# Wider value products, one GLU block moved, and a token-major end in a two-layer hybrid encoder

## The chip, the cores and the metric

The kernel runs on one core of a Trainium2 chip. The metric is the device time of one execution in microseconds (us). The engines are named as the profile names them: PE is TensorE's matrix products (PEld its weight loads), DVE is VectorE, ACT is ScalarE, POOL is GpSimd, SP is SyncE, whose queue issues most DMA transfers.

## The reference, cut to what matters

All is float32, with 512 tokens, width 1024 and two layers. The heads of the neighbourhood attention and the two halves of the GLU are columns of one projection.

```python
h = rmsnorm(x, norm_mix[i])
proj = h @ w_in[i]
qa, ka, va, glu_in, qc, kc, vc, gates = jnp.split(proj, SPLITS, axis=-1)
ya = diff_attention(qa, ka, va, ...)              # 4 heads of 2 x 64, values of 128
yb = conformer_conv(glu_in, ...)                  # a * sigmoid(g), 31 taps per channel, layernorm, silu
yc = neighbourhood_attention(qc, kc, vc, rpb)     # 8 heads of 64, window 8 x 16 on an 8 x 64 grid
merged = ga * (ya @ w_br_a) + gb * (yb @ w_br_b) + gc * (yc @ w_br_c)
x = x + merged @ w_o[i]
x = x + (silu(h @ w_ffn_gate[i]) * (h @ w_ffn_up[i])) @ w_ffn_down[i]     # h: normed x
x = x + sigmoid(h @ w_ple_gate[i]) * (p[i] @ w_ple_in[i])                 # h: normed x
# after both layers: rmsnorm(x, norm_final)
```

## The kernel before

Activations lie channel-major: a tile has 128 channels on the partitions and 512 tokens along them, and the width of 1024 is eight such chunks. Every product is made of three: both operands are split into a rounded high part and the rest (`split`: ACT writes `hi`, DVE writes `lo`), and PE adds hi·hi, hi·lo and lo·hi in PSUM (`mm3`, lines 175 to 177). `weights` loads 128 x 1024 raw weights over SP's queue into a `wr` buffer (two of them), and splits them into `wh` and `wl` (three each).

PE's instructions run in the order in which the program writes them. On the other engines a scheduler orders by priority; `weights` raises its own, so that loads and splits run ahead. Each engine works its queue in order. DMA transfers use eight semaphores in turn: a transfer waits until the one eight before it has landed.

The attention work is woven into the products by hand. `chunk` counts steps of a product (three products of 512 columns each), and every fourth step is a tick, about 2.7 us of PE time. `later(gen, delay, gap)` puts a piece of work on a list that starts `delay` ticks later and at least `gap` ticks after the one before; its `yield n` continues n ticks on. A `natten_unit` makes the scores of one head and half of the queries, the softmax (DVE and ACT), two ticks later the transposes, and two ticks later the attention output. `background(after, n)` puts n of the 124 convolution taps per layer (DVE, line 158, `conv_z`) behind an instruction; the numbers stand in `BG`.

A layer begins with the GLU. In layer 0 `opening` loads x and the weights of the first four blocks in pieces, after ten warm-up products (line 321), and multiplies chunk by chunk as they land. The products are made from x before its root mean square is known; DVE multiplies by the row factor (`rb`) afterwards, and `scaled` makes normalised operands (`hs`) for all later products. `glu` makes four pairs of blocks, j = 0 to 3, each a gate and a value. Then come `natten_in(pr)` for four pairs of heads (q and k, whose halves are stacked by DMA copies, `stack`, line 617), and `natten_v(g)` for two groups of four heads: `values` (lines 571 to 575) takes 128 tokens of `hs` as the stationary operand and 256 columns of weights as the moving one.

PSUM has eight banks: `mm` three, `sc` two, `tr` two, `av` one.

At the end `ple` makes eight blocks of the embedding gate. The eighth goes through `final`, in two halves of 256 tokens: products, gate, the sum of squares by products with ones, a power on POOL, and, because the output is token-major, transposes of all eight chunks. Each 128 tokens are scaled by their factor (lines 1048 and following) and stored as one transfer of 128 x 1024.

Of the kernel before, what the change touches and what calls it, by code (L numbers as in the profile page):

```python
# [20 lines left out]
P = 128  # L21
L = 2
# [8 lines left out]
CONV_W = 31  # L31
HALO = CONV_W // 2
# [13 lines left out]
PAR_L = 8 + 8 + 8 + 1 + 4 + 4 + 4 + 4 * CONV_W  # L46
PAR = L * PAR_L + 8
WARM = 10
BG = dict(glu=2, natten=3, diff=1, gatec=2, branchc=1, gateb=5, mergea=4, mergea2=2)
# [10 lines left out]
class Net:  # L60
# [99 lines left out]
    def split(self, hi, lo, src):  # L160
        self.act(hi, src, AF.Copy)
        self.tt(lo, src, hi.bitcast(F32), ALU.subtract)

    def weights(self, ap, n):
        with self.tc.high_priority(offset=min(self.w_ahead, self.tc.cur_priority - self.p0)):
            raw = self.sb("wr", [P, 1024])
            hi = self.sb("wh", [P, 1024], F32R)
            lo = self.sb("wl", [P, 1024], F32R)
            self.nc.sync.dma_start(raw[:, :n], ap[:, :n])
            self.split(hi[:, :n], lo[:, :n], raw[:, :n])  # L170
        return hi, lo
# [135 lines left out]
    def opening(self):  # L307
# [4 lines left out]
        mix = slice(0, KD)  # L312
        nc.scalar.dma_start(self.parts[:, mix], a["par"][:, mix])
# [3 lines left out]
        nc.scalar.dma_start(xc[1], a["xT"][1])  # L317
        nc.scalar.dma_start(self.parts[:, KD:], a["par"][:, KD:])
        warm = self.ps("av")
        for _ in range(WARM):  # L320
# [4 lines left out]
        raws = {"t": [self.sb("t", [P, 256]) for _ in range(4)],  # L325
                "rp": [self.sb("rp", [P, 256]) for _ in range(4)],
# [8 lines left out]
        for k in range(KD):  # L335
            if k > 1:
                nc.sync.dma_start(xc[k], a["xT"][k])
            pieces = {0: (0, 256, "t"), 2: (256, 512, "rp"), 4: (512, 1024, "e")}
            if k == 0:
                h.append(self.operand(xc[k], self.par(0, "mix", k), FIRST[0][k]))  # L340
            if k in pieces:
                c0, c1, tag = pieces[k]
                for m, (src, wh, wl, _) in enumerate(blocks):
                    raw = raws[tag][m]
                    nc.sync.dma_start(raw, src[:, c0:c1])
                    self.split(wh[:, c0:c1], wl[:, c0:c1], raw)
            if k:
                h.append(self.operand(xc[k], self.par(0, "mix", k), FIRST[0][k]))
# [62 lines left out]
    def layer(self, i, h, xsrc, xs):  # L411
# [53 lines left out]
    def glu(self, zs):  # L465
# [5 lines left out]
        for j in range(4):  # L471
# [12 lines left out]
            def value(j=j, pa=pa, sg=sg, ta=ta, z=z):  # L484
                self.tt(ta, pa, self.rb, ALU.mult)
                mid = z[:, HALO:HALO + GW, :]
                zc = self.tt(mid.rearrange("p a b -> p (a b)"), ta, sg, ALU.mult)
                nc.vector.memset(z[:, 0:HALO, 0:1], 0.0)
                nc.vector.memset(z[:, HALO + GW:, GR - 1:GR], 0.0)
                nc.vector.tensor_copy(z[:, 0:HALO, 1:GR], z[:, GW:GW + HALO, 0:GR - 1])  # L490
                nc.vector.tensor_copy(z[:, HALO + GW:, 0:GR - 1], z[:, HALO:2 * HALO, 1:GR])
# [3 lines left out]
            self.ready(value)  # L495

    def taps(self, zs, cs):

        for j, z in enumerate(zs):
# [3 lines left out]
            for d in range(CONV_W):  # L503
                w = self.par(self.i, "cw", j * CONV_W + d)
# [83 lines left out]
    def natten_in(self, pr, st, ys):  # L588
# [19 lines left out]
        for n in range(4):  # L608
            self.later(self.natten_unit(pr, n // 2, n % 2, st4, k2, st, box, ys[pr]), 5, 1)
# [10 lines left out]
    def natten_v(self, g, st):  # L620
# [3 lines left out]

        def parts(v, a):
            v = v.rearrange("p (u a b c) -> p u a b c", u=2, b=2, c=64)
            a = a.rearrange("p (u a c) -> p u a c", u=2, c=64)
            return [(v[:, u, :, u], v[:, u, :, 1 - u], a[:, u]) for u in range(2)]

        vs = self.values(self.a["w_vc"][self.i, g], parts)  # L630


        vd = self.sb("x", [P, 2, 512], F32R)
        for n, edge in enumerate((vs[1][0:64, 0], vs[0][64:P, 1])):
            for o in range(0, P, 64):
                self.nc.sync.dma_start(vd[o:o + 64, n].bitcast(F32), edge.bitcast(F32))
        st["v", g] = vs, vd

    def natten_unit(self, pr, half, u, st4, k2, st, box, y):
# [55 lines left out]
        hc = u * 256 + (pr % 2) * P  # L695
# [253 lines left out]
    def ple(self, h, x, xs, pairs):  # L949
# [4 lines left out]
        for m in range(KD - last):  # L954
# [17 lines left out]
            self.ready(gate)  # L972
            if m >= EARLY:
# [15 lines left out]
        if last:  # L989
            return self.final(h, x[KD - 1], pairs, hn, st[0])  # L990
        self.i = i + 1
        self.main_norm(st[0], (3, 2), x=x)
        return hn

    def final(self, h, x, pairs, hn, most):
# [3 lines left out]
        nc, i, m = self.nc, self.i, KD - 1  # L999
        wg = self.weights(self.a["w_pg"][i, m], 1024)  # L1000
        wi = self.weights(self.a["w_pi"][i, m], 256)
        hn.append(self.sb("h", [P, 512]))
        g = self.sb("t", [P, 512])
        sq = self.sb("t", [P, 512])
        sums = self.ps("tr", (P, 2, 4))

        def products(out, w, acts, half, ks):
            s = slice(half * 256, half * 256 + 256)
            for k in ks:
                a = acts[k] if isinstance(acts[k], tuple) else (acts[k][:, 0, :], acts[k][:, 1, :])  # L1010
                c = slice(k * P, (k + 1) * P)
                self.mm3(out, w[0][:, c], w[1][:, c], a[0][:, s], a[1][:, s],
                         k == 0, k == len(acts) - 1)

        def total(n, src, cs):
            for c in cs:
                nc.tensor.matmul(sums[:, n, c:c + 1], src[:, c * P:(c + 1) * P],
                                 self.ones[:, 0:1], start=True, stop=True)

        def turn(tag, n, c):  # L1020
            o = self.ps(tag, (P, 4, P))
            for u in range(4):
                nc.tensor.transpose(o[:, u], hn[4 * n + u][:, c * P:(c + 1) * P], self.ident)
            return o.rearrange("p a b -> p (a b)")

        def gate(pg, half):
            s = slice(half * 256, half * 256 + 256)
            self.tt(g[:, s], pg, self.rb[:, s], ALU.mult)
            self.act(g[:, s], g[:, s], AF.Sigmoid, table="sigmoid")

        def rest(pi, half):
            s = slice(half * 256, half * 256 + 256)
            self.tt(g[:, s], g[:, s], pi, ALU.mult)
            self.tt(x[:, s], x[:, s], g[:, s], ALU.add)
            self.act(sq[:, s], x[:, s], AF.Square)
            self.act(hn[m][:, s], x[:, s], AF.Copy, scale=self.par(0, "fin", m))

        def column(half):
            cs = slice(2 * half, 2 * half + 2)
            ms = self.sb("sm", [P, 2])  # L1040
            self.stt(ms, sums[:, 1, cs], 1.0 / D, part[:, cs], ALU.mult, ALU.add)
            col = self.sb("rc", [P, 2])
            nc.gpsimd.tensor_tensor(col, ms, self.power[:, 0:2], ALU.pow)
            return col

        def store(c, col, tiles):
            r = rows[c]
            nc.vector.tensor_scalar(r[:, 0:512], tiles[0], col, None, ALU.mult)
            self.act(r[:, 512:1024], tiles[1], AF.Copy, scale=col)
            nc.sync.dma_start(self.a["out"][c * P:(c + 1) * P, :], r)  # L1050

        rows = [t for _ in range(2) for t in self.parts_of("qk", [1024], 2)]
        pg = [self.ps("mm", (P, 256)), None]
        products(pg[0], wg, h, 0, range(8))
        gate(pg[0], 0)
        pi = [self.ps("sc", (P, 256)), None]
        products(pi[0], wi, pairs, 0, range(2))
        rest(pi[0], 0)
        total(0, most, range(4))
        part = self.sb("sm", [P, 4])  # L1060
        nc.vector.tensor_scalar(part, sums[:, 0, :], 1.0 / D, EPS, ALU.mult, ALU.add)
        lows = [turn("av", 0, 0), turn("tr", 0, 1)]
        pg[1] = self.ps("mm", (P, 256))
        products(pg[1], wg, h, 1, range(6))
        total(1, sq, (0, 1))
        col = column(0)
        products(pg[1], wg, h, 1, range(6, 8))
        gate(pg[1], 1)
        pi[1] = self.ps("sc", (P, 256))
        products(pi[1], wi, pairs, 1, range(2))  # L1070
        rest(pi[1], 1)
        for c in range(2):
            store(c, col[:, c:c + 1], (lows[c], turn("mm", 1, c)))
        lows = [turn("sc", 0, 2), turn("sc", 0, 3)]
        total(1, sq, (2, 3))
        col = column(1)
        highs = [turn(t, 1, 2 + c) for c, t in enumerate(("mm", "av"))]
        for c in range(2):
            store(2 + c, col[:, c:c + 1], (lows[c], highs[c]))
# [17 lines left out]
def _heads(w):  # L1097

    w = w.reshape(L, D, 2, 2, 2, 64).transpose(0, 1, 2, 4, 3, 5)
# [89 lines left out]
```

## Time and profile before

| What | Value |
|---|---|
| median of 3 runs | 1832.29 us (1831.8 to 1832.62) |
| the profiled execution | 1832.66 us |
| its span, first to last instruction | 1830.6 us |
| mean granted TensorE clock | 0.998 |
| PE / DVE / ACT busy | 1815.6 / 1190.5 / 764.8 us |
| layer 0: values of natten, first and last product | 64.4 and 120.9 us |
| last PE work | about 1824.7 us |

A row of a busy-time window reads: the window, its length, then for each engine its busy time and the number of instructions, then the granted clock as a share of full speed, the DMA engines' share, and GB/s. A row of the waits reads: engine, tile and line, who released it, total us, times, longest. A row of the timeline reads: start, duration, engine, line, operation, output<-inputs.

### The profile page before, as it was taken

What the parts mean: (1) busy time and instruction counts of PE and PEld (TensorE: products, weight loads), DVE (VectorE), ACT (ScalarE), POOL (GpSimd) and SP (SyncE); (2) the same over time, 40 slices, a digit from 0 to 9 for tenths busy, and PEclk for the clock granted to TensorE, in tenths of its full rate; (3) what the DMA queues carried; (4) which work ended last, traced back from release to release, by engine and by line L of the source; (5) the groups of instructions that cost most, each with busy time, mean ns of one, the idle gap of its engine ahead of it and who ended that gap; (6) DMA issues with size and microseconds to landing.
All of it is one profiled execution on the core that took longest, in us unless ns stands there. A gap on an engine that the chain in (4) does not pass through costs nothing.

```text
span 1830.6 us, 23574 instructions
## 1 busy us (share of the span) xinstructions
PE 1815.6 (99%) x8796; PEld 1524.3 (83%) x8796; DVE 1190.5 (65%) x1917; ACT 764.8 (42%) x1330; POOL 23.6 (1%) x56
## 2 busy tenths in 40 slices
PE   9999999999999999999999999999999999999998
PEld 7888888888888888888888888888878888888887
DVE  6888887887644434445777878888775444344455
ACT  5476555325432222233535755552353322232344
POOL 0000000000000000000000000000000000000000
PEclk9999999999999999999999999999999999999999
DMA  5565541334422232223436655322353222322232
GB/s 176 176 191 167 144 135 41 109 101 156 146 98 99 82 102 103 99 81 113 152 121 203 183 156 145 103 75 93 107 193 104 99 97 79 117 92 99 84 107 102
DMA packets 88225, 221.13 MB, mean 121 GB/s; under 512 B 12080, under 2 KB 19376, under 8 KB 88112
## 3 DMA queue, kind: packets, MB, share of 16 engines
q1 hardware_dynamic: 87536, 218.94, 37.5%
q8 instruction: 70, 1.15, 0.2%
q10 hardware_dynamic: 576, 0.69, 0.1%
q14 instruction: 43, 0.35, 0.1%
HBM read 180.79 MB, written 7.34 MB: 103 GB/s over the span
## 4 chain that ended last, share of the span: by engine, by line
PE 93%; DVE 2%; DMA 2%; ACT 2%; issue 1%; DVEq 0%; ACTq 0%; SPq 0%; POOLq 0%; POOL 0%
PE ffn_mm L175 13%; PE ffn_mm L177 13%; PE ffn_mm L176 13%; PE mergea_mm L176 2%; PE mergea_mm L175 2%; PE mergea_mm L177 2%; PE diff_sc L757 2%; PE gatec_mm L175 2%; PE gatec_mm L176 2%; PE gatec_mm L177 2%; PE ple_mm L177 2%; PE ple_mm L175 2%; PE ple_mm L176 2%; PE wo_mm L176 2%; PE wo_mm L177 2%; PE diff_mm L175 2%
## 5 line engine op out<-in xcount | busy, mean ns | idle before, releaser
L141 ACT ACTIVATE ffn_wh<-ffn_wr 128x1024 fp32r<-128x1024 f32 (+1 forms) x152 | 144.0, 949 | 513.9 <-issue 367.8
L175 PE MATMUL ffn_mm<-wo_h,ffn_wh 128*128 128x512 f32 x704 | 274.2, 390 | 0.0
L177 PE MATMUL ffn_mm<-wo_h,ffn_wl 128*128 128x512 f32 x704 | 273.9, 389 | 0.0
L176 PE MATMUL ffn_mm<-wo_h,ffn_wh 128*128 128x512 f32 x704 | 273.9, 389 | 0.0
L155 DVE TENSOR_TENSOR ffn_wl<-ffn_wr,ffn_wh 128x1024 fp32r<-128x1024 f32 (+1 forms) x152 | 164.7, 1085 | 129.2 <-ACT ffn_wh L141 129.2
L158 DVE SCALAR_TENSOR_TENSOR conv_z<-glu_z,pre_par,conv_z 128x512 f32<-128x512 f32 x240 | 179.4, 748 | 3.0
L177 PEld LDWEIGHTS ffn_mm<-wo_h,ffn_wl 128*128 128x128 f32 x704 | 132.1, 188 | 27.5
L176 PEld LDWEIGHTS ffn_mm<-wo_h,ffn_wh 128*128 128x128 f32 x704 | 132.1, 188 | 27.4
L175 PEld LDWEIGHTS ffn_mm<-wo_h,ffn_wh 128*128 128x128 f32 x704 | 132.1, 188 | 27.3
L155 DVE TENSOR_TENSOR ffn_t<-ffn_t,ffn_mm 128x512 f32<-128x512 f32 x44 | 30.3, 688 | 114.8 <-PE ffn_mm L177 114.8
L155 DVE TENSOR_TENSOR ffn_t<-ffn_mm,wo_r 128x512 f32<-128x512 f32 x44 | 30.4, 691 | 110.3 <-PE ffn_mm L177 110.3
L141 ACT ACTIVATE mergea_wh<-mergea_wr 128x1024 fp32r<-128x1024 f32 (+1 forms) x32 | 27.1, 848 | 96.6 <-PE mergea_mm L176 70.8
L175 PE MATMUL ffn_mm<-ffn_z,ffn_wh 128*128 128x512 f32 x160 | 62.2, 389 | 0.0
L176 PE MATMUL ffn_mm<-ffn_z,ffn_wh 128*128 128x512 f32 x160 | 62.2, 389 | 0.0
L177 PE MATMUL ffn_mm<-ffn_z,ffn_wl 128*128 128x512 f32 x160 | 62.2, 389 | 0.0
L175 PE MATMUL ffn_mm<-ffn_y,ffn_wh 128*128 128x512 f32 x160 | 62.2, 389 | 0.0
L176 PE MATMUL ffn_mm<-ffn_y,ffn_wh 128*128 128x512 f32 x160 | 62.2, 389 | 0.0
L177 PE MATMUL ffn_mm<-ffn_y,ffn_wl 128*128 128x512 f32 x160 | 62.2, 389 | 0.0
L141 ACT ACTIVATE diff_a<-diff_sc,diff_s 128x512 f32<-128x512 f32 x32 | 22.0, 689 | 61.8 <-DVE diff_s L848 61.8
L848 DVE TENSOR_REDUCE diff_s<-diff_sc 128x1 f32<-128x512 f32 x64 | 41.9, 685 | 5.9 <-PE diff_sc L757 5.8
L155 DVE TENSOR_TENSOR wo_x<-wo_x,ffn_mm 128x512 f32<-128x512 f32 x32 | 22.0, 687 | 31.5 <-PE ffn_mm L177 31.5
L141 ACT ACTIVATE natten_wh<-natten_wr 128x1024 fp32r<-128x1024 f32 x24 | 25.4, 1056 | 37.4 <-issue 18.0
(583 smaller groups left out, 4628.6 us busy)
## 6 DMA issues: line engine op xcount, KB each, us to landing
ffn_wr<-w_fg SPq DMA_DIRECT2D x44, 512.0 KB, 3.2
ffn_wr<-w_fu SPq DMA_DIRECT2D x44, 512.0 KB, 3.1
ffn_wr<-w_fd SPq DMA_DIRECT2D x32, 512.0 KB, 3.4
natten_wr<-w_in SPq DMA_DIRECT2D x16, 512.0 KB, 3.7
natten_b<-bias SPq DMA_DIRECT2D x32, 256.0 KB, 3.3
diff_wr<-w_in SPq DMA_DIRECT2D x16, 512.0 KB, 3.5
gatec_wr<-w_in SPq DMA_DIRECT2D x16, 512.0 KB, 4.0
gateb_wr<-w_in SPq DMA_DIRECT2D x16, 512.0 KB, 3.3
```

The lines of the kernel that those rows point to most:

```text
L141: i = self.nc.scalar.activation(out, in_, func, **kw)
L155: return self.nc.vector.tensor_tensor(out, a, b, op)
L158: return self.nc.vector.scalar_tensor_tensor(out, a, s, b, op0, op1)
L175: mm(out, wh, ah, start=first, stop=False)
L176: mm(out, wh, al, start=False, stop=False)
L177: mm(out, wl, ah, start=False, stop=last)
L757: self.nc.tensor.matmul(out, st4[:, u, qs], st[:, ks], start=n == 0, stop=n == 1)
L848: nc.vector.tensor_reduce(out=m[:, u:u + 1], in_=sc, op=ALU.max, axis=AX.X, negate=True)
```

## The change

Values: `natten_v` makes the values of all eight heads at once. For each of the eight chunks and each 128 tokens it makes products of 512 columns into four banks (two `mm`, `av`, one `sc`). The weights are laid out wide (`_wide`), and the four banks are evicted in eight splits of 256 columns. Three taps go behind each weight split.

GLU: `glu` makes three pairs. The fourth (`glu_last`) is made from `hs`, its gate between the second and third pair of heads and its value between the third and fourth, with the sigmoid read straight from PSUM. The first pair of heads is due 10 ticks after its k instead of 5.

Opening: x's first chunk is the first transfer on SP's queue. The first weight pieces have 128 and 384 columns instead of 256 and 256; the first of them goes over ACT's queue.

End: the last two blocks are token-major. For each 128 tokens, the stationary operand is the activations and the moving one is the weights of both blocks side by side (256 columns). The sum of squares of these columns is made by DVE, the gain of the two blocks is applied as a row (`gains`), and each 128 tokens are stored by two transfers, one on ACT's queue and one on SP's.

Buffers: `wr` 3 instead of 2, `t` 7 instead of 8, `r` 3 instead of 4. A constant is renamed.

```diff
-BG = dict(glu=2, natten=3, diff=1, gatec=2, branchc=1, gateb=5, mergea=4, mergea2=2)
+BG = dict(glu=2, natten=1, values=3, diff=1, gatec=2, branchc=2, gateb=4, mergea=4, mergea2=2)
...
-        self.bufs = dict(wr=2, wh=3, wl=3, h=8, qk=2, kh=2, v=4, pt=2, y=5, z=5, x=4, t=8, rp=4,
-                         e=4, a=3, r=4, ss=1, sm=8, rc=4, b=2, s=8)
+        self.bufs = dict(wr=3, wh=3, wl=3, h=8, qk=2, kh=2, v=4, pt=2, y=5, z=5, x=4, t=7, rp=4,
+                         e=4, a=3, r=3, ss=1, sm=8, rc=4, b=2, s=8)
...
+        nc.sync.dma_start(xc[0], a["xT"][0])
         nc.scalar.dma_start(self.parts[:, mix], a["par"][:, mix])
-        xc = [t for _ in range(KD // 2) for t in self.parts_of("x", [512], 2)]
-        nc.scalar.dma_start(xc[0], a["xT"][0])
         self.consts()
...
-            pieces = {0: (0, 256, "t"), 2: (256, 512, "rp"), 4: (512, 1024, "e")}
+            pieces = {0: (0, P, "t"), 1: (P, 512, "rp"), 4: (512, 1024, "e")}
             if k == 0:
+                nc.scalar.dma_start(raws["t"][0], blocks[0][0][:, 0:P])
+                nc.scalar.dma_start(xc[1], a["xT"][1])
+                nc.scalar.dma_start(self.parts[:, KD:], a["par"][:, KD:])
...
-        self.natten_v(0, sn)
+        self.natten_v(sn)
+        last = self.glu_last(zs)
         self.natten_in(1, sn, yc)
+        next(last)
         self.natten_in(2, sn, yc)
-        self.natten_v(1, sn)
+        next(last)
         self.natten_in(3, sn, yc)
...
-        for j in range(4):
+        for j in range(3):
...
+    def glu_last(self, zs):
+        self.phase = "glu"
+        sg = self.sb("t", [P, 512])
+        z = self.sb("z", [P, GW + 2 * HALO, GR])
+        self.act(sg, self.proj(OFF_GLU + CB + 3 * P), AF.Sigmoid, table="sigmoid")
+        yield
+        self.phase = "glu"
+        self.gated(z, self.proj(OFF_GLU + 3 * P), sg)
+        zs.append(z)
+        yield
...
-            self.later(self.natten_unit(pr, n // 2, n % 2, st4, k2, st, box, ys[pr]), 5, 1)
+            self.later(self.natten_unit(pr, n // 2, n % 2, st4, k2, st, box, ys[pr]), 5 if pr else 10, 1)
...
+        accs = [self.ps(t) for t in ("mm", "mm", "av", "sc")]
+        for o in range(0, KD, 2):
+            wh, wl = self.weights(self.a["w_vc"][self.i][:, o * 512:(o + 2) * 512], 1024)
+            self.background(self.low, self.bg["values"])
+            for k in (o, o + 1):
+                s = slice((k - o) * 512, (k - o + 1) * 512)
+                for t, out in enumerate(accs):
+                    hi, lo = (a[:, t * P:(t + 1) * P] for a in self.halves(self.h[k]))
+                    mm(out, hi, wh[:, s], start=k == 0, stop=False)
+                    mm(out, hi, wl[:, s], start=False, stop=False)
+                    mm(out, lo, wh[:, s], start=False, stop=k == KD - 1)
+                    self.chunk()
...
-        for m in range(KD - last):
+        for m in range(KD - 2 * last):
...
+        for t in range(4):
+            pg = self.ps("mm", (P, 256))
+            if t == 0:
+                inputs(0)
+                inputs(1)
+            products(pg, wg, h, t, range(4))
+            if t == 1:
+                chunks(0)
+            if t in (1, 2):
+                low.append(turn(places[t - 1], hn[0:4], t - 1))
+            products(pg, wg, h, t, range(4, 6))
...
+            if t:
+                chunks(t)
+            if t > 1:
+                inputs(t)
+            products(pg, wg, h, t, range(6, 8))
+            pgs.append(pg)
+            if t == 1:
+                finish(0)
+            if t:
+                finish(t)
+            if t in (1, 2):
+                store(t - 1)
+        for t in (2, 3):
+            low.append(turn(places[t], hn[0:4], t))
+            store(t)
```

In `final`, `inputs` and `products` are the products of the embedding and of the gate for 128 tokens, `chunks` and `turn` transpose finished chunks into `tr` and other banks, `finish` is the sigmoid, the gated sum, its squares and the power, and `store` scales the rows and issues the two transfers.

More of the change, by code (lines that the diff above doesn't have):

```diff
@@ L169, in weights @@
             self.nc.sync.dma_start(raw[:, :n], ap[:, :n])
[L170 removed]
+            self.low = self.split(hi[:, :n], lo[:, :n], raw[:, :n])
         return hi, lo
@@ L972, in ple @@
             self.ready(gate)
+            if last and m == 3:
+                self.gains()
             if m >= EARLY:
@@ L993, in ple, with gains @@
         return hn
-    def final(self, h, x, pairs, hn, most):
[L999 to L1008, printed above, removed]
-            for k in ks:
[L1010 to L1020, printed above, removed]
+    def gains(self):
+        o = self.ps("tr", (P, 2, P))
+        for u in range(2):
+            g = self.par(0, "fin", KD - 2 + u)
+            self.nc.tensor.transpose(o[:, u], g.to_broadcast([P, P]), self.ident)
+        self.gain = self.sb("b", [P, 2 * P])
+        self.act(self.gain, o.rearrange("p a b -> p (a b)"), AF.Copy)
@@ L1021, in turn @@
             o = self.ps(tag, (P, 4, P))
-            for u in range(4):
-                nc.tensor.transpose(o[:, u], hn[4 * n + u][:, c * P:(c + 1) * P], self.ident)
+            for u, a in enumerate(src):
+                nc.tensor.transpose(o[:, u], a[:, t * P:(t + 1) * P], self.ident)
             return o.rearrange("p a b -> p (a b)")
[L1026 to L1079, printed above, removed]
+        def finish(t):
+            g = self.sb("t", [P, 256])
+            self.act(g, pgs[t], AF.Sigmoid, table="sigmoid", scale=rbs[:, t:t + 1])
+            self.tt(g, g, pis[t], ALU.mult)
+            v = self.sb("a", [P, 256])
+            self.tt(v, g, pair[t][:, 256:], ALU.add)
+            q = self.sb("t", [P, 256])
+            s = self.sb("s", [P, 1])
+            nc.vector.tensor_tensor_reduce(
+                out=q, in0=v, in1=v, scale=1.0, scalar=0.0, op0=ALU.mult, op1=ALU.add,
+                accum_out=s)
+            ms = self.sb("sm", [P, 1])
+            self.stt(ms, s, 1.0 / D, part[:, t:t + 1], ALU.mult, ALU.add)
+            col = self.sb("rc", [P, 1])
+            nc.gpsimd.tensor_tensor(col, ms, self.power[:, 0:1], ALU.pow)
+            vs.append(v)
+            columns.append(col)
@@ new lines, in store @@
+        def store(t):
+            col, two = columns[t], pair[t]
+            r, out = rows[t], self.a["out"][t * P:(t + 1) * P]
+            self.act(r[:, 0:512], low[t], AF.Copy, scale=col)
+            nc.scalar.dma_start(out[:, 0:512], r[:, 0:512])
+            self.stt(r[:, 768:], vs[t], col, self.gain, ALU.mult, ALU.mult)
+            nc.vector.tensor_scalar(r[:, 512:768], two[:, 0:256], col, None, ALU.mult)
+            nc.sync.dma_start(out[:, 512:], r[:, 512:])
+        pair, low, pgs, vs, columns = [], [], [], [], []
@@ new lines, in final, with inputs, chunks @@
+        places = ("av", "mm", "av", "sc")
+        def inputs(t):
+            pis.append(self.ps("sc", (P, 256)))
+            products(pis[t], wi, pairs, t, range(2))
+        def chunks(t):
+            pair.append(turn("tr", (hn[4], hn[5], x[0], x[1]), t))
+        pis = []
+        for t in range(4):
[10 more added lines that the diff above has]
+            if t == 1:
+                sums = self.ps("mm", (P, 4))
+                for c in range(4):
+                    mm(sums[:, c:c + 1], most[:, c * P:(c + 1) * P], self.ones[:, 0:1],
+                       start=True, stop=True)
+                part = self.sb("sm", [P, 4])
+                nc.vector.tensor_scalar(part, sums, 1.0 / D, EPS, ALU.mult, ALU.add)
+            if t:
[4 more added lines that the diff above has]
+            pgs.append(pg)
+            if t == 1:
+                finish(0)
[3 more added lines that the diff above has]
+                store(t - 1)
```

102 lines of the change are left out of this document (64 added, 38 removed).

## The prediction

> **What bounds the kernel now.** I read the page first, then PE's waits, then windows of busy time, then the timeline.
>
> ```profile
> span 1830.6 us, 23574 instructions
> PE 1815.6 (99%) x8796; PEld 1524.3 (83%) x8796; DVE 1190.5 (65%) x1917; ACT 764.8 (42%) x1330; POOL 23.6 (1%) x56
> PE 93%; DVE 2%; DMA 2%; ACT 2%; issue 1%; DVEq 0%; ACTq 0%; SPq 0%; POOLq 0%; POOL 0%
> ```
>
> PE (TensorE) is busy 99% and is 93% of the chain that ended last. So time can leave only where PE's own work shrinks, where PE waits, where its clock is low, and after its last product.
>
> PE's waits (us in total, times, longest):
>
> ```profile
> PE natten_sc L757 <- DMA natten_x<-natten_t: 2.0, 1, 2.0
> PE pre_mm L175 <- ACT pre_y L141: 1.4, 1, 1.4
> PE natten_tr L678 <- DVE natten_pt L155: 1.3, 2, 0.6
> PE natten_av L699 <- DVE natten_y L155: 0.7, 3, 0.3
> ```
>
> Busy time by window; the granted clock stands before the DMA share:
>
> ```profile
> 4.70:8.11 3.41, 2.00 (x8) 1.05 (x7) 1.73 (x5) 2.49 (x7) 0.00 (x0) 1.00 1.06 371
> 8.11:11.53 3.42, 3.42 (x10) 2.68 (x9) 3.42 (x11) 3.21 (x9) 0.00 (x0) 0.50 0.97 248
> 82.00:140.00 58.00, 55.52 (x351) 48.95 (x349) 46.90 (x118) 40.68 (x106) 1.51 (x10) 1.00 0.68 192
> 308.50:333.00 24.50, 24.50 (x121) 20.49 (x119) 22.03 (x34) 10.33 (x17) 1.39 (x1) 1.00 0.32 108
> ```
>
> PE worked only 2.00 of the 3.41 us before 8.11, and in the next 3.42 us it was granted half its clock. That window is a loss of 1.7 us.
>
> The pitch of the products, from the timeline (start, duration):
>
> ```profile
> 63.74 0.39 PE L175 MATMUL natten_mm<-glu_b,natten_wh 128*128 128x512 f32 x1
> 63.97 0.39 PE L176 MATMUL natten_mm<-glu_b,natten_wh 128*128 128x512 f32 x1
> ...
> 64.79 0.28 PE L571 MATMUL natten_mm<-natten_wh,glu_h 128*128 128x256 f32 x1
> 64.91 0.28 PE L573 MATMUL natten_mm<-natten_wl,glu_h 128*128 128x256 f32 x1
> 65.03 0.28 PE L575 MATMUL natten_mm<-natten_wh,glu_h 128*128 128x256 f32 x1
> ```
>
> Start to start, a 512-column product takes 0.2275 us (24 of them 5.46) and a 256-column one 0.120 us. The durations overlap and are not the cost.
>
> The profiled execution took 1832.66 us, 2.1 more than its span and 0.37 above the median of 1832.29. The sum is made on 1832.66 and moved by 0.37 at the end.
>
> **Values, 512 columns.** Per layer 192 products of 256 columns become 96 of 512: 23.04 us become 21.84. Over two layers that is −2.4 us, all on PE, which has no other work to hide it. The Trainium skill, "TensorE: Matmul & The Clock Gate", section "Wait — 56ns, not 53.3ns?", gives N ÷ 2.4 GHz plus about 2.5 ns from start to start. By that estimate the two forms cost 20.97 and 20.72 us per layer, and the whole part would bring 0.5 us; the trace's 0.120 and 0.2275 disagree, and I take the trace. The evictions (16 ACT and 16 DVE pieces per layer at 0.28) become 8 and 8 of double width, about 0.4 each by the 256-wide rows. They lie under the next pair's first product (5.46 us); its second product wants the first value bank, free after about 1.6 us. If that cover went, it would cost up to 5 us per layer.
>
> **First scores.** In layer 0 the first scores wait 2.02 us for the copies that stack k. The values of all heads (21.84 us) now stand between k and these scores, and the first pair's units are due 10 ticks after k instead of 5. The copies have landed by then: −2.0. The other natten waits sum to 2.0 us. I take nothing off them.
>
> **Opening.** Before: x's first chunk is second on ACT's queue behind 128 rows of 32 bytes, issued 1.17, landed 5.22; the first operand starts 5.62, PE's first real product 6.70, and the first 96 products end at 30.78 (24.1 us for 21.84 us of work, because of the half clock). After: the chunk is first on SP's queue. The nearest row is SP's first transfer, issued 0.74 and landed 3.31 (128 KB; the chunk is 256 KB). I take 3.6 to 4.4; the far end is the old 5.22. ACT's queue still holds, ahead of the first operand, the issue of the remaining parameters, which waits for that chunk (0.33). Then come the operand (0.63 to the next start) and a 128-column split (about 0.3). First product possible at 4.9 to 5.7. But PE is in its ten warm-up products until 5.33 (last start 4.90, 0.43 each), so it goes from warm-up into work with almost no idle time, and the reason for the half clock is gone. The second chunk needs pieces of 384 columns. Up to the last of them 1.54 MB must land; the DMA view has 0.42 MB moved by 4.0 us and then 349 to 392 GB/s, which gives 7.1, some 7.6 with the landing. PE gets there at 8.1. 5.4 + 21.84 + 0.3 for small waits = 27.5: −3.2. Bounds: 0 (chunk as late as before) to −3.5; a loss is excluded, since all that PE needs is issued no later than before.
>
> **GLU block moved.** 48 products per layer change place, nothing on PE. Two multiplications by the row factor (0.69, DVE) go. ACT gains two table loads per layer (9 loads become 13), 1.28 each by the row at 301.90, with the next activation 10 ns later. The Trainium skill, "ScalarE: Activation LUTs", "What ACT_TABLE_LOAD costs", adds a drain of about 1.38 us; the trace shows none. Behind the sigmoid, which waits for its product, ACT holds splits of attention outputs and the next exponentials. But each block brings 5.46 us of products, so ACT has more time, not less; the load at 983.80 stood in this stage with PE full. Bounds 0 to 5.1; I take +0.2.
>
> In layer 0 the stage now starts 10.9 us sooner after the row factor. The second value bank is the one that q of the first pair leaves, and DVE frees it after 18 us of queued work (factor, two GLU blocks, three weight splits, rescaled chunks), at about 50 to 51; PE wants it at 50.9. Bounds 0 to 1.5; +0.2.
>
> **Background taps.** Fewer in the natten stage (DVE 46.9 of 58.0 there now), 8 more per layer in branchc: 22.03 + 8 × 0.67 = 27.4 us in 24.5. The backlog of 2.9 us drains in gateb (4 instead of 5), and weight splits run two blocks (5.5 us) ahead, so PE should not see it. Bounds 0 to 2.9 per layer; +0.3 for both.
>
> **Third raw buffer, smaller `t` and `r`.** PE shows no wait for a weight split, so earlier loads bring nothing; `r`'s four uses per layer are long apart. 0; without that cover, the wait would be at SP's queue, with copies of k and v behind it, and those have over 10 us.
>
> **Tail.** From block 5's last product (1803.9) to the end it takes 26.7 us. New: 120 products of 256 columns 14.4 us, against 14.0 (30 of 512, 60 of 256); before the last one also 24 transposes at 0.11 and 8 single-column sums 0.9: 18.1. Then one chain for the last 128 tokens:
>
> ```profile
> 1823.78 0.17 DVE ple_sm L158
> 1823.99 0.07 issue
> 1824.06 0.73 POOLq L1182
> 1824.81 0.75 DVE ple_qk L1048
> ```
>
> Sigmoid 0.42, DVE's leftovers of the third store up to 0.5, two adds and multiplies 0.84, square-sum 0.50, the mean 0.17, POOL 0.73, two half rows 0.85: 4.0 with hand-overs. The store was 2.6 from issue to landing for 512 KB, now two of 256 KB: 2.5. Then 1.06 to the end. 18.1 + 7.6 + 0.2 for two gain transposes = 25.9: −0.8. Bounds −1.8 to +1.0 (PE waiting for the two `tr` banks).
>
> **Sum.** −2.4 −2.0 −3.2 +0.2 +0.2 +0.3 −0.8 = −7.7: 1832.66 − 7.7 − 0.37 = about 1824.5.
>
> **Rivals.**
> Half clock stays. If the chunk lands late, or PE idles between the splits, the 8.11 window stays at 0.5 and the opening brings 3.2 − 1.7 − 0.3 = 1.2: 1826.5. For it: the clock followed idle time once already. Against: 5.33 covers most of the chunk's range. The Trainium skill, "TensorE: Matmul & The Clock Gate", "Part 1: The HAM clock gate", says that the 3.4 us window runs free of the kernel's start; by that rule the half-rate stretch may also fall elsewhere in another execution. The traces so far show one execution only, with the stretch behind the idle time.
> Covers lost. DVE late for the banks, branchc behind, values' evictions seen: +1.5, +2.5, +0.5 on the sum gives 1829. For it: DVE is at 90% in branchc. Against: PE has no wait there now.
> No gain by the wider product. If a 512-column product with the activations stationary costs two of 256 (0.240), the values bring 0: 1826.9. No row has this form; against it, every row of 512 columns here has the same pitch, whatever is stationary.
> Slower: softmax falls behind. If the sigmoid holds ACT's queue so that all 32 units' transposes wait 0.4 us (longest now 0.6), that is 12.8: 1837. It decides once ACT needs more than a unit's PE time; it is busy 40.7 of 58.0, and two loads add 2.6. Little speaks for it.
> That the change fails to do what it says is excluded by the built program: 96 products of 512, x first on SP.
>
> **How the numbers follow.** Forecast 0.58; half clock 0.17; covers lost 0.13; no wider gain 0.04; slower 0.08. About 0.2% (3.7 us) is what a measurement here can tell from no change: faster is below 1828.6, slower above 1836.0. Faster: 0.58, 0.15 of the half clock, 0.04 of the covers and 0.04, together 0.81; the rest of these two is the same, 0.11; slower 0.08. The low end takes the opening −3.5, tail −1.8 and half of the other natten waits: 1821. The high end takes in the covers lost: 1830.
>
> **What would show it.** PEclk 1.00 in every window from 4.7 on and glu_tr near 27.5; values 21.8 us per layer; no wait at the first scores; end about 26 us after block 5. Wrong if PE's waits in natten or branchc sum to over 5 us, or if glu_tr stays past 29.

## The result and the profile after

The changed kernel takes 1821.5 us (median of 6 runs, 1820.96 to 1822.57), the kernel before 1832.05 (6 runs, 1830.91 to 1834.95). The ratio is 0.9942, with a 95% interval of 0.9929 to 0.9955. The profiled execution took 1821.5, and its span fell from 1830.6 to 1819.7. The forecast was 1824.5; the gain is 10.6, where 7.7 had been summed up.

From the page after:

```profile
span 1819.7 us, 23245 instructions
...
PE 1807.6 (99%) x8628; PEld 1513.9 (83%) x8628; DVE 1187.8 (65%) x1908; ACT 768.9 (42%) x1313; POOL 25.2 (1%) x58
...
PE 94%; DVE 2%; ACT 2%; DMA 1%; issue 0%; SPq 0%; POOLq 0%; DVEq 0%; ACTq 0%
```

PE is still the bound: its busy time fell by 8.0 us and the span by 10.9. PE's waits after (us in total, times, longest):

```profile
PE natten_av L731 <- DVE natten_y L155: 4.1, 8, 0.8
PE pre_av L319 <- DVE pre_zeror L381: 1.1, 1, 1.1
PE pre_mm L176 <- DVE glu_v L158: 0.2, 1, 0.2
PE pre_mm L175 <- ACT pre_y L141: 0.2, 1, 0.2
```

The wait of the first scores (2.0) is gone. A wait of the attention output for the eviction of its one bank grew from 0.7 to 4.1. Busy time by window, the granted clock ahead of the DMA share:

```profile
4.70:8.11 3.41, 3.41 (x15) 2.74 (x14) 2.77 (x7) 1.95 (x5) 0.00 (x0) 1.00 0.93 272
8.11:11.53 3.42, 3.26 (x14) 2.20 (x13) 1.79 (x6) 2.80 (x6) 0.00 (x0) 1.00 1.07 360
82.00:140.00 58.00, 57.35 (x317) 48.65 (x316) 40.70 (x105) 42.99 (x103) 1.52 (x10) 1.00 0.71 191
302.60:327.10 24.50, 24.50 (x120) 20.53 (x119) 24.17 (x38) 10.45 (x18) 1.50 (x1) 1.00 0.33 108
```

The half-clock window is gone. In the third row DVE has 40.7 us of work where it had 46.9. In the fourth (branchc) it is full, 24.17 of 24.5, and PE does not wait.

By stage, from the two timelines, the span fell by 2.1 us up to glu_tr (30.62 to 28.50), 3.8 in the rest of layer 0, 3.3 in layer 1 up to block 5's last product and 1.6 behind it.

### The profile page after: what moved, and what is told of

The parts are those of the page before. It is cut to its first block, busy times and chain, and to the rows that moved or that the text cites. A ratio compares the mean times of both kernels' runs of the same rounds, so it can differ in the third digit from the quotient of the medians.

```text
span 1819.7 us, 23245 instructions
## 1 busy us (share of the span) xinstructions
PE 1807.6 (99%) x8628; PEld 1513.9 (83%) x8628; DVE 1187.8 (65%) x1908; ACT 768.9 (42%) x1313; POOL 25.2 (1%) x58
## 4 chain that ended last, share of the span: by engine, by line
PE 94%; DVE 2%; ACT 2%; DMA 1%; issue 0%; SPq 0%; POOLq 0%; DVEq 0%; ACTq 0%
PE ffn_mm L175 13%; PE ffn_mm L176 13%; PE ffn_mm L177 13%; PE mergea_mm L176 2%; PE mergea_mm L175 2%; PE mergea_mm L177 2%; PE diff_sc L789 2%; PE gatec_mm L175 2%; PE gatec_mm L176 2%; PE gatec_mm L177 2%; PE gateb_mm L176 2%; PE gateb_mm L175 2%; PE wo_mm L175 2%; PE gateb_mm L177 2%; PE wo_mm L176 2%; PE wo_mm L177 2%
```

## Experiments

Each kernel starts from the changed kernel unless its text says otherwise. The first table sets PE's waits in natten and diff, summed from the waits of each profile, beside the windows of 3.41 us at half clock inside the run. The text reads the rows afterwards. Between the first two rows the waits hardly differ: the 10.6 us between them come from elsewhere, from the values, the opening, the end and two waits of layer 1.

| kernel | median us | ratio to before, 95% | waits in natten and diff, us | half-clock windows |
|---|---|---|---|---|
| before | 1832.05 | | 4.3 | 1 (opening) |
| changed | 1821.50 | 0.9929 to 0.9955 | 4.1 | 0 |
| old tap numbers | 1833.74 | 1.0001 to 1.0018 | 11.9 | 1 |
| two raw buffers | 1834.24 | 1.0005 to 1.0022 | 14.5 | 1 |
| units first | 1820.19 | 0.9925 to 0.9950 | 2.6 | 0 |
| units first, two raw buffers | 1821.36 | 0.9931 to 0.9956 | 3.2 | 0 |
| units first, old tap numbers | 1820.57 | 0.9928 to 0.9956 | 2.9 | 0 |
| units first, GLU not moved | 1827.59 | 0.9973 to 0.9991 | 8.6 | 2 |
| before, three raw buffers | 1829.15 | 0.9975 to 0.9993 | 3.8 | 1 |
| before, units first | 1839.81 | 1.0036 to 1.0062 | 11.9 | 4 |

**Opening undone.**

```diff
-        nc.sync.dma_start(xc[0], a["xT"][0])        # x first, 128 + 384 columns
+        nc.scalar.dma_start(xc[0], a["xT"][0])      # behind par, 256 + 256 columns
```

> The changed kernel with the opening of before (x's first chunk second on ACT's queue, pieces of 256 and 256 columns). Theory: the opening's gain is the earlier first product plus the half-clock window that followed PE's idle time. Then the first real product is back at 6.7 us (after: 5.49), PE idles 1.4 us behind the warm-ups, a window at half clock follows, glu_tr is back at 30.6 (after: 28.50), and the time is 1821.5 + 2.1 = 1823.6. Rival: the half-clock window of before did not come from the idle time but from where the clock's window happened to fall. Then PEclk stays at 1.00 behind the first product, glu_tr is at about 29.4, and the time is 1822.4.

Measured: 1823.23 us (1822.35 to 1824.18), ratio 0.9940 to 0.9967; span 0.7 us longer than after. The first product is back at 6.70, but glu_tr (the work that follows the opening's products) comes at 29.06, and no window at half clock follows the idle time:

```profile
4.70:8.11 3.41, 2.39 (x8) 1.14 (x7) 1.73 (x5) 2.49 (x7) 0.00 (x0) 1.00 1.02 362
8.11:11.53 3.42, 3.42 (x17) 2.83 (x16) 3.37 (x11) 3.38 (x9) 0.00 (x0) 1.00 0.96 297
```

PE does 17 products in the second window, against 10 at half clock in the profile before. In the trace the rival held: of the 2.1 us between the profiles of before and after, the new opening brings 0.6 and the other 1.6 is a half-clock window that one profiled execution had. Even the 0.6 is uncertain: over the nine profiles of kernels with the new opening glu_tr comes between 28.23 and 28.90, and over the three with the old opening and full clock between 28.86 and 29.07. Their means differ by 0.3.

The median does not decide for the rival: 1823.23 lies nearer to the theory's 1823.6 than to 1822.4. The profiled execution is the fastest of its five, and whether the others had the window isn't known.

Three profiles with the opening of before (this one and the two variants of before, below) did not have the window there. Of the 51 executions of before that were timed beside the experiments, 15 had a mean granted clock of 0.997 or 0.998, as the profiled one had, and 36 one of 0.999 or 1.000; the spans of the first are 1.6 us longer on average. One such window takes 1.7 us. That fits a window in a minority of the executions, but the mean clock does not say where in an execution the clock was low.

**End undone.**

```diff
-            return self.final(h, x[KD - 2:], pairs, hn, st[0])     # two blocks token-major
+            return self.final(h, x[KD - 1], pairs, hn, st[0])      # the eighth, in halves
```

> The changed kernel with the end of before (seven channel-major blocks and the eighth in two halves). Theory: the new end is worth all of the 1.6 us by which the distance from block 5's last product to the end of the span fell (26.66 to 25.02), so it goes back to 26.7 and the time to 1823.1. Rival: my step of 0.8 was right and the rest was where the two executions differ otherwise: 25.8 and 1822.3.

Measured: 1822.87 us (1822.41 to 1823.44), 0.9938 to 0.9963. From the start of block 5's last product to the end of the span it takes 26.87 us in before and 26.91 here, against 25.25 in the changed kernel and within 0.01 of that in the nine other runs with the new end. So the new end is worth 1.6 to 1.7 us in the traces, the theory's number; the medians differ by 1.4.

**Values in two halves.**

```diff
-                    mm(out, hi, wh[:, s], start=k == 0, stop=False)
...
+                    for a, b, i0, i1 in ((hi, wh, k == 0, 0), (hi, wl, 0, 0), (lo, wh, 0, k == KD - 1)):
+                        for c in range(2):
+                            mm(out[:, c * 256:c * 256 + 256], a,
+                               b[:, s.start + c * 256:s.start + c * 256 + 256],
...
```

> The changed kernel with each 512-column product of the values made as two of 256 columns into the same bank, with the same weights, banks and evictions. Theory: by the pitches of before (0.120 and 0.2275 us) the stage from the first to the last value product grows from 21.84 to 23.04 us in each layer, 2.4 us in all: 1823.9. By the page's estimate (N over 2.4 GHz plus 2.5 ns) it grows by 0.25 per layer: 1822.0. Since the extra instructions also shift the scheduler's priorities, the rest of the time may move by itself; the stage's own length decides.

Measured: 1824.17 us (1823.66 to 1824.27), 0.9947 to 0.9971, 2.7 over the changed kernel. From the first to the last start the value products take 23.00 and 22.91 us in the two layers, against 21.68 and 21.55. The pitches of the traces give the cost. The estimate from the Trainium skill ("TensorE: Matmul & The Clock Gate", "Wait — 56ns, not 53.3ns?") would have put it at 0.5. The rest of the time did not move.

**Old tap numbers, and two raw buffers.** Two runs, each undoing one edit that the prediction had put at +0.3 or at nothing:

```diff
-BG = dict(glu=2, natten=1, values=3, diff=1, gatec=2, branchc=2, gateb=4, ...)
+BG = dict(glu=2, natten=3, values=0, diff=1, gatec=2, branchc=1, gateb=5, ...)
```

> The changed kernel with the numbers of background taps of before (natten 3, values 0, branchc 1, gateb 5). Theory: two waits of layer 1 that I had not counted (before pin_sc 0.6 and before wo_mm 0.5, with the products stretched around them 1.1 to 1.8 us) vanished because gateb puts four taps in front of DVE's work instead of five; then they return, natten's DVE work grows, the waits of natten_av for natten_y (4.1) grow to 5 or more, and the time is 1821.5 + 1.5 + 1 = 1824. Rival: the tap numbers are off PE's path and the third raw buffer removed these waits; then no wait of over 0.3 shows at pin_sc and wo_mm and the time is 1821.5 within 0.5.

```diff
-        self.bufs = dict(wr=3, ...
+        self.bufs = dict(wr=2, ...
```

> The changed kernel with two raw weight buffers instead of three. Theory: weight splits run ahead of PE with two as well; PE's waits stay as in the changed kernel (4.1 us at natten_av, none at pin_sc or wo_mm) and the time is 1821.5 within 0.5. Rival: the third buffer took away layer 1's waits before pin_sc and wo_mm; then they return and the time is 1822.6 to 1823.3.

Measured: 1833.74 (1831.39 to 1835.96) and 1834.24 us (1833.25 to 1836.02). Both theories were wrong, and so were both rivals: either edit alone gives back the whole gain, and more, mostly at places that neither text names. The two waits before pin_sc and wo_mm, which had caught the eye in layer 1, do not return. The waits with the old tap numbers, then with two raw buffers:

```profile
PE natten_sc L789 <- DVE natten_s L686: 3.8, 2, 1.9
PE natten_av L731 <- DVE natten_y L155: 3.7, 7, 1.2
PE natten_tr L712 <- ACT natten_e L141: 2.1, 2, 1.0
PE natten_tr L710 <- ACT natten_e L141: 1.6, 2, 0.8
```

```profile
PE natten_tr L710 <- ACT natten_e L141: 5.3, 2, 2.7
PE natten_av L731 <- DVE natten_y L155: 4.9, 6, 1.8
PE natten_sc L789 <- DVE natten_s L686: 3.8, 2, 1.9
```

No row waits for a weight. All of these rows are steps of the attention units. With two raw buffers the longer waits (10.4 us) and the half-clock window (1.7) make 12.1 of the 12.7 us; with the old tap numbers (7.8 and 1.7) they make 9.5 of 12.2, and the rest stands in no row. The order on DVE shows how such a wait comes about. First the changed kernel (timeline of DVE; start, duration), around the unit whose scores wait:

```profile
156.33 0.42 DVE L686 CUSTOM_DVE_ANT_0 natten_b<-natten_sc,natten_b 128x256 f32<-128x256 f32 x1 [1.01 <-PE natten_sc L789]
...
158.10 0.43 DVE L155 TENSOR_TENSOR natten_y<-natten_av,natten_y 64x256 fp32r<-64x256 f32 x1
158.56 0.42 DVE L686 CUSTOM_DVE_ANT_0 natten_b<-natten_sc,natten_b 128x256 f32<-128x256 f32 x1
...
158.91 0.69 DVE L155 TENSOR_TENSOR diff_rp<-diff_rp,diff_r 128x512 f32<-128x512 f32 x1
159.52 0.75 DVE L158 SCALAR_TENSOR_TENSOR conv_z<-glu_z,pre_par,conv_z 128x512 f32<-128x512 f32 x1
```

and with two raw buffers:

```profile
157.59 0.42 DVE L686 CUSTOM_DVE_ANT_0 natten_b<-natten_sc,natten_b 128x256 f32<-128x256 f32 x1 [1.02 <-PE natten_sc L789]
...
159.24 0.69 DVE L155 TENSOR_TENSOR diff_rp<-diff_rp,diff_r 128x512 f32<-128x512 f32 x1
159.84 0.75 DVE L158 SCALAR_TENSOR_TENSOR conv_z<-glu_z,pre_par,conv_z 128x512 f32<-128x512 f32 x1
160.50 0.69 DVE L155 TENSOR_TENSOR diff_rp<-diff_rp,diff_r 128x512 f32<-128x512 f32 x1
161.22 0.43 DVE L155 TENSOR_TENSOR natten_y<-natten_av,natten_y 64x256 fp32r<-64x256 f32 x1
161.68 0.69 DVE L155 TENSOR_TENSOR diff_rp<-diff_rp,diff_rp 128x512 f32<-128x512 f32 x1
162.40 0.42 DVE L155 TENSOR_TENSOR natten_y<-natten_y,natten_av 64x256 fp32r<-64x256 f32 x1
162.85 0.42 DVE L686 CUSTOM_DVE_ANT_0 natten_b<-natten_sc,natten_b 128x256 f32<-128x256 f32 x1
```

The step that frees a score bank (`natten_b`, line 686) stood ahead of the rotary steps of diff (`diff_rp`) and the tap; now it stands behind them and comes 4.3 us later, though the same unit's first such step is only 1.3 late (156.33 and 157.59). PE's next scores show it:

```profile
163.34 0.39 PE L789 MATMUL natten_sc<-natten_qk 128*128 128x256 f32 x1 [1.90 <-DVE natten_s L686]
```

PE's own order is the same in both kernels, and so is it with the old tap numbers; DVE, ACT and SP do the same instructions too, and only the order that the scheduler wrote for these three differs. That this order, and not the buffer itself, is the cause was the next theory.

**Units first.** In `natten_unit`, the three pieces between the `yield`s get a priority:

```diff
+        with self.tc.high_priority(offset=100):
             for t in range(2):      # scores, softmax
...
+        with self.tc.high_priority(offset=100):
             pt = self.ps("tr", (P, 2, 256))      # transposes and their splits
...
+        with self.tc.high_priority(offset=100):
             vs, vd = st["v", pr // 2]      # attention output and its splits
```

It ran with two raw buffers, with three, and with the old tap numbers:

> The run with two raw buffers cost 12.7 us, which I had put at nothing. Here it runs again, with one addition: in natten_unit the steps of the softmax, the transposed splits and the splits of the attention output get a priority of 100, so that the program's scheduler places them on DVE's and ACT's queues ahead of the rotary steps of diff and of background taps. Theory: the third raw buffer matters because it changes the order in which the scheduler fills DVE's and ACT's queues, with the units' steps late; not because weights land late. Then PE's waits in natten and diff fall from 14.5 us to under 6, and the time is 1819 to 1822 with two buffers. Rival: the splits wait for the weights, whose loads wait for a free raw buffer; then the order helps little and the time stays at 1830 to 1834.

> The changed kernel with the same priority of 100 for the units' steps, and its three raw buffers. Theory: the new waits of natten_av for natten_y (4.1 us in 8) come from rotary steps of diff that stand on DVE's queue ahead of the eviction; with the units first they fall to 1.5 or less and the time is 1821.5 - 2.6 = about 1819. Rival: DVE is so full here (16.4 of 20 us) that what is set back is wanted at once: PE then waits for weight splits or for the copies of diff, and the time is 1821.5 to 1824.

> The tap numbers of before in the changed kernel cost 12.2 us. Here they stand with the units' steps first (priority 100, three raw buffers). Theory: the tap numbers, like the raw buffers, act through the order on DVE's and ACT's queues; with the units first the waits of natten_sc, natten_tr and natten_av (11.9 us) fall to under 5 and the time is 1820 to 1823.5. Rival: natten's twelve more taps are work that DVE has no time for there; then at least half of the loss stays, 1826 or more, with PE waiting for weight splits or units.

Measured: 1821.36 us (1820.56 to 1821.64), 1820.19 (1819.62 to 1820.58) and 1820.57 (1819.76 to 1820.88). The theory of the order held three times: with the units first, two raw buffers cost 1.2 us instead of 12.7, and the old tap numbers 0.4 instead of 12.2. With two raw buffers, the two steps that free the score banks now follow each other ahead of the tap:

```profile
158.14 0.42 DVE L687 CUSTOM_DVE_ANT_0 natten_b<-natten_sc,natten_b 128x256 f32<-128x256 f32 x1
...
158.49 0.42 DVE L687 CUSTOM_DVE_ANT_0 natten_b<-natten_sc,natten_b 128x256 f32<-128x256 f32 x1
...
159.40 0.75 DVE L158 SCALAR_TENSOR_TENSOR conv_z<-glu_z,pre_par,conv_z 128x512 f32<-128x512 f32 x1
```

In the changed kernel itself the waits for `natten_y` fall from 4.1 to 1.0:

```profile
PE natten_av L734 <- DVE natten_y L155: 1.0, 4, 0.3
PE natten_tr L712 <- DVE natten_pt L155: 0.9, 2, 0.4
PE natten_tr L714 <- DVE natten_pt L155: 0.7, 1, 0.7
```

The span is 1.2 us shorter than the changed kernel's, where 2.6 was expected, and the waits in natten and diff are 1.5 less. The intervals of the two ratios overlap, so the times alone don't tell the two apart.

**Before with three raw buffers, and before with the units first.** The same two edits in the old kernel:

> The kernel before with three raw weight buffers, t 7 and r 3, and nothing else. Theory: a third buffer brings nothing by itself, it only lets the scheduler make another order, which for the work of before may be better or worse: 1832 within 3, with PE's waits moved to other places in natten and diff and no wait for a weight. Rival: the third buffer is itself worth the 12.7 us that its loss costs the changed kernel: 1820 to 1824, with the excess of PE's pitch in natten and diff down from 10.7 to under 5.

> The kernel before with the units' steps first and nothing else. Theory: its excess over PE's pitch in natten and diff (10.7 us in both layers) is only partly of that order: the 2.0 us of the first scores wait for copies and stay, the waits for natten_pt, natten_y and natten_s (2.3 us) shrink, and the time is 1829 to 1831.5. Rival: the queue order is the whole difference between the two kernels outside the values; then the time is near 1826.

Measured: 1829.15 us (1826.14 to 1830.88) and 1839.81 (1839.45 to 1840.87). The third buffer's theory held, though at the edge of its 3 us: against the runs of before beside it (1831.57) a gain of 2.4, not of 12.7. Layer 1's two waits went (pin_sc, wo_mm, 1.1 us), while the first scores wait twice for copies, 1.0 each, and the one half-clock window stands behind these waits and not in the opening.

The units-first text was wrong on both sides: the old kernel becomes 8.9 us slower than the runs of before beside it (1830.89).

```profile
PE natten_mm L175 <- DVE natten_v L155: 7.7, 2, 3.8
PE natten_sc L760 <- DMA natten_x<-natten_t: 1.9, 1, 1.9
PE natten_av L702 <- DVE natten_y L155: 1.9, 3, 0.8
```

Here the second group's values are made between the units, and their evictions (`natten_v`), set back behind the units, hold the banks that the next pair's products want. The changed kernel makes all values ahead of the units and has no such wait.

**GLU not moved, units first.**

```diff
-        for j in range(3):
+        for j in range(4):
...
-        last = self.glu_last(zs)
...
-        next(last)
```

> The run with the units first (1820.2), with the fourth GLU block back at the start with the other three. Theory: moving the block was worth little for PE either way (I took +0.2); the time is 1819.5 to 1821 and ACT's table loads fall from 13 to 9. Rival: the moved block gives the units time, since its products stand between the pairs of heads; without it, PE waits more for them, and the time is 1823 or more.

Measured: 1827.59 us (1826.32 to 1828.7). The rival held: 7.4 us. The table loads fall from 13 to 9, and PE waits:

```profile
PE natten_av L731 <- DVE natten_y L155: 8.6, 10, 2.5
```

The longest wait falls in a stage of diff, and the next 3.41 us are granted half the clock, in each layer:

```profile
157.32:160.73 3.41, 0.88 (x8) 0.70 (x7) 3.25 (x8) 1.64 (x5) 0.00 (x0) 1.00 0.68 219
160.73:164.14 3.41, 3.41 (x17) 3.41 (x18) 2.64 (x8) 2.35 (x6) 0.15 (x1) 0.50 0.59 166
```

A likely reason, which was argued and not tested: without the block's 10.9 us of products between the pairs of heads, more of the last units falls beside diff's rotary steps. What the move is worth without the priority was not tried.

**Opening again.** Units first, with two edits:

```diff
-WARM = 10
+WARM = 8
...
-                nc.scalar.dma_start(self.parts[:, KD:], a["par"][:, KD:])      # at k == 0
+            if k == 3:
+                nc.scalar.dma_start(self.parts[:, KD:], a["par"][:, KD:])
```

> The run with the units first, with two edits in the opening: eight warm-up products instead of ten, and the remaining parameters loaded behind the fourth chunk's products instead of ahead of the first operand. Theory: the first product starts when its operands are there (about 4.8 us) instead of when the warm-ups end (5.5), the pieces of 384 columns land sooner because 165 KB of small rows no longer go ahead of them, and glu_tr comes at 27.3 to 27.8 instead of 28.5: about 1819.3. Rival: the pieces' landing sets the pace of the first chunks, and PE waits out what it gains: glu_tr at 28.3 or later and 1820.2.

Measured: 1819.47 us (1818.49 to 1820.02), 0.9924 to 0.9949, and glu_tr at 28.40. By glu_tr the rival held, though the median lies nearer to the theory's 1819.3: the first product starts at 4.63, against 5.32 in the run with the units first alone, but the first ones run at half clock and PE still waits for the second chunk. glu_tr comes 0.35 sooner (28.75 to 28.40), which is less than it varies between runs with the same opening. The kernel has the lowest median of all here, 2.0 us under the changed one; the intervals of their ratios overlap.

## Why the prediction came out right, and where it was wrong

The sum had the sign and most of the size, and that it came within 3 us is in part luck: the opening was overpriced, the end and the values were underpriced, two waits of layer 1 went without a term, and the order of the queues, which alone could cost 12 us, turned out well. Its terms:

| step | predicted | runs |
|---|---|---|
| values, 512 columns | −2.4 | −2.7 (values in halves) |
| first scores | −2.0 | wait of 2.0 gone in the trace; no run of its own |
| opening | −3.2 | −0.3 to −0.6, and −1.6 that was the clock, in the traces; −1.7 by the medians (opening undone) |
| GLU block moved | +0.2 | −7.4 with the units first |
| taps | +0.3 | −12.2; −0.4 with the units first |
| third raw buffer | 0 | −12.7; −1.2 with the units first, −2.4 in the kernel before (there with the smaller `t` and `r`) |
| end | −0.8 | −1.6 (end undone) |

The runs' numbers do not add up to the gain, since what one of these edits is worth depends on the others. No run undid the smaller `t` and `r` alone.

Two sums of the prediction do not come out. The terms that it names for its low end (0.3 of the opening, 1.0 of the tail, 1.0 of waits below the sum) give 1822.2 and not 1821: the measured 1821.5 lies inside the range as written, and just below what those terms reach. And PE's part of the tail, 14.4 + 2.6 + 0.9, is 17.9 and not 18.1.

*Values, first scores.* Right in mechanism and size. The evictions stayed covered: no wait for a value bank shows. For the first scores the mechanism rests on the trace alone.

*Opening.* Two steps failed. The half clock was taken as a consequence of the late chunk, worth 1.7, and its removal counted in full; but the same opening ran without it. Counting windows of 3.41 us from the first full clock, PE was busy for 0.59 of the idle window in before, and half clock followed; in the three other profiles with that opening it was 0.64, 0.70 and 0.79, and none followed. So the idle time looks like a condition, and how much of it fell into one window seems to have decided. The new opening removes the idle time; how often that saves the 1.7 us is open. And the second chunk's pieces were to land by 7.6 at 349 to 392 GB/s; the window 4.70 to 8.11 moved 272, and PE stretched its products and waited at 9.3 and 12.2, so glu_tr came at 28.5 and not at 27.5. The first product, forecast at 5.4, came at 5.49, at the end of the warm-ups, as forecast. The rule that the clock's window runs free of the kernel's start (the Trainium skill, "TensorE: Matmul & The Clock Gate", "Part 1: The HAM clock gate") fits: full clock is first granted at 4.70 in before and between 4.00 and 7.13 in the other runs.

*End.* The mechanism held, the chain was priced too high. From the chain of waits, the rows that answer to those of before:

```profile
1814.60 0.17 DVE ple_sm L158
...
1814.81 0.07 issue
1814.88 0.58 POOLq L1246
...
1815.48 0.48 DVE ple_y L158
```

POOL's step took 0.58 instead of 0.73, DVE's leftovers of the third store (0.5) were done before the sigmoid ended, and the chain behind the last product took 7.0 us instead of 7.6. PE's part before it took 18.0 instead of 18.3.

*GLU, taps, third buffer.* Here the working failed, though the sum hid it. The prediction looked for a cover for each (ACT's time, DVE's backlog, weight waits), found one, and put 0 to +0.3. It left out that each edit changes the order in which the scheduler fills DVE's and ACT's queues, and that in natten and diff PE waits for single steps there: the one that frees a score bank, the exponentials, the eviction of `av`. The rival "softmax falls behind", at 0.08, came nearest to what decided, though by another route: it had the sigmoid holding ACT's queue, while here rotary steps, taps and weight splits stand ahead of the units' steps. In the changed kernel that did not come, and with either edit undone it did: 1833.7 and 1834.2 against the rival's 1837. The priced quantity was how busy an engine is; what mattered was what stands ahead of one instruction.

*Not foreseen.* The waits before pin_sc and wo_mm in layer 1 (0.6 and 0.5, with the stretched products about 1.4) are gone in all other kernels here but one: before with the units first waits for `mergeb_v` at wo_mm (0.4, in layer 0). They went in before with a third buffer and did not return with two, so they too seem to hang on the order. Which edit took them away in the changed kernel stays open. The 4.1 us at `natten_av` were under the bound of 5 that the prediction had set for natten.

*The rivals.* No gain by the wider product: out, by the run in halves. Covers lost: the bank, branchc and the evictions show no wait. The table loads cost no drain: the load at 980.87 takes 1.28 and the next activation starts at 982.17.

## What to carry to other kernels

When a scheduler fills in-order queues, an edit to buffer counts or background work is also an edit to the order. Find the few steps that free what PE wants next, look in the new order at what stands ahead of them, and price that as a range of its own, here up to 12.7 us, even where every engine has time. Then fix these steps by a priority: here it cut the cost of two such edits from over 12 us to about 1, though with it the place of one GLU block was still worth 7.4. And check which evictions the priority sets back, for it cost the older kernel 8.9 us.

A term that one profiled execution shows only once (a half-clock window) should not be counted in full as the gain of the edit that stands beside it.

## What the runs showed of the hardware

PE's clock falls for 3.41 us, and sometimes twice that, behind a window of the same length in which PE had little to do, in the middle of the kernel too. Over the runs, counting the grid of 3.41 us windows from the first full one, the windows before each half-clock one inside a run had PE busy for 0.26 to 0.59 of their length. Windows of 0.61 and more were never followed by half clock; some of 0.43 to 0.55 were not either. So a wait of some 2.5 us can cost a further 1.7: the two waits of the run with GLU not moved are 2.5 each, and each is followed by such a window.
